# Squares behind the first norm, the second norm's product behind more tiles, rotation tables inside the FFN

## The chip, the cores and the metric

The kernel runs on 1 core of one Trainium2 chip. The metric is the time of one execution in device microseconds (us), taken as the median of several runs; lower is better. TensorE (PE) is shown with one of two granted clock levels, 1.2 and 2.4 GHz; a granted clock of 1.00 in a table means 2.4 GHz throughout, 0.50 would mean 1.2 GHz throughout.

## What is computed

Two transformer blocks follow each other on a sequence of 512 tokens with 1024 features, each with two layers, and each layer is a mixer and then a feed-forward part (FFN). Both parts have a norm ahead of them and a norm behind them, so between any two parts stands the same pair: the post-norm of what the part gave, added to the stream `x`, and the pre-norm of `x` for the next part.

```python
h = rms_norm(x, mix_norm_pre[l]) * (1.0 + sc_m) + sh_m
y = hybrid_mixer(h, positions, ...)
x = x + g_m * rms_norm(y, mix_norm_post[l])
h = rms_norm(x, ffn_norm_pre[l]) * (1.0 + sc_f) + sh_f
y = swiglu(h, w_gate_up[l], w_down[l])
x = x + g_f * rms_norm(y, ffn_norm_post[l])
```

The second block does the same without the scale and shift, with another mixer (`hybrid_mixer_2`) and a convolution in its FFN. `rms_norm` divides by the root of the mean square over the 1024 features. Both mixers rotate queries and keys by tables of cosine and sine of the positions; the second block has positions of its own (`positions_2`).

## The kernel before

Features lie on the 128 partitions, so `x` is eight tiles `x[k]` of 128x512, and tokens lie along the row. A weight is loaded in pieces of 128x1024 (`load`, L257 to L268): SyncE issues a DMA into `raw` (4 buffers), ScalarE rounds it to `whi` (L265), VectorE subtracts to get the rest, `wlo` (L267); there are four buffers each of `whi` and `wlo`. Every product of a weight and an activation is three matmuls: high by high, high by low, low by high.

At a boundary between two parts the work is cut into two halves of 256 tokens (A and B, `HALVES`). The last product of a part (`out_proj` for a mixer, `down2` for an FFN) runs its first output tiles whole and the others by half (`in_halves`): all of them for half A, then in reverse order for half B. So half A is done first and its norms can run while PE works on half B. The next part starts with `fm_split`: some output tiles for half A, then the same tiles for half B. The places where the norms stand between these tiles are given by small numbers at the top of the file: `LA` (mixer to FFN) and `LB` (FFN to mixer) say before which of the half-B tiles half A's pre-norm stands; `LC` (FFN) and `LD` (mixer) say before which half-A tile of the next part half B's pre-norm stands. A half-A or half-B tile of `out_proj` or `fm_split` is 24 matmuls, one of `down2` 33.

`post_norm` (L475) sums the squares of `y` over the partitions by a product with a matrix of ones (`nrm`), takes the root on ScalarE (`rstd`), and VectorE makes `yn` and adds it to `x`. `pre_norm` (L437) squares `x` on ScalarE (L444), adds pairs on VectorE (L446), has four products with ones on PE, takes the root, and then makes `xn` (VectorE), `hh` (ScalarE) and `hl` (VectorE), eight of each, which the next part's matmuls read. `rope_tables` (L544) makes the rotation tables: for the second block it is called right ahead of the FFN of the first block's second layer.

A scheduler puts the recorded instructions of each engine in an order by its own reckoning; on the chip each engine then runs its row as it stands and waits on semaphores. There are seven such boundaries with a following part: four from a mixer to an FFN, three from an FFN to a mixer.

Of the kernel before, what the change touches and what calls it, by code (L numbers as in the profile page):

```python
# [13 lines left out]
AF = mybir.ActivationFunctionType  # L14
ALU = mybir.AluOpType
# [6 lines left out]
KT = D // P  # L22
# [16 lines left out]
PD1 = 0  # L39
PD2 = 0  # L40
EARLY = 6
PAIRS = 4
PH1 = 0
PH2 = 0
PXM = 0
SA = 0
LA = 2
LAG = 3
LOA = 40
NO = 7  # L50
LB = 1
LC = 4
LD = 2
WIN = 0
KF = 3
KM = 1
# [20 lines left out]
HALVES = (slice(0, 256), slice(256, 512))  # L77
# [31 lines left out]
def steps(it, n):  # L109
    for _ in range(n):  # L110
        next(it, None)
        yield


def seq(*parts):
    for p in parts:
        yield from p
# [12 lines left out]
def run(steps):  # L130

    while True:
        try:
            dbg(steps)
            next(steps)
        except StopIteration as e:
            return e.value
# [49 lines left out]
class Net:  # L187
# [174 lines left out]
    def norms(self, y, sqs, g, nxt, late):  # L362


        if nxt is None:
            steps = [lambda i=i: self.post_norm(HALVES[i], y, sqs, g, True) for i in range(2)]
            return {0: steps[0]}, steps[1], (None, None)
        h = self.new_h()
        post = [lambda i=i: self.post_norm(HALVES[i], y, sqs, g) for i in range(2)]
        pre = [lambda i=i: self.pre_norm(HALVES[i], *nxt, *h) for i in range(2)]  # L370
        self.pending = pre[1]
        if late == 0:
            return {0: lambda: (post[0](), pre[0]())}, post[1], h
        return {0: post[0], late: pre[0]}, post[1], h

    def fm_split(self, chunks, act, pool, more=None):

        tiles = [self.ps("pj" if i < PJ else "ps") for i, _ in enumerate(chunks)]  # L380

        begin = {LC if more is None else LD: self.pending}
        middle = {} if more is None else {0: lambda: run(steps(more, 4))}
        self.in_halves([(i, [src]) for i, src in enumerate(chunks)], KF if more is None else KM,
                       lambda i, ws, hs, _: self.fm(tiles[i], ws[0], 0, act, hs, range(KT)), pool,
                       begin, middle)
        return tiles
# [46 lines left out]
        run(self.tok_steps(*args))  # L434


    def pre_norm(self, hs, gs, sh, hh, hl):  # L437

        nc, x = self.nc, self.x
        ps = self.ps("nrm")  # L440
        sq = None
        for k in range(KT):
            s2 = self.half("sq")
            nc.scalar.activation(s2, x[k][:, hs], AF.Square)  # L444
            if sq is not None:
                nc.vector.tensor_tensor(s2, sq, s2, ALU.add)  # L446

            sq = s2 if k < 2 * PAIRS and k % 2 == 0 else None
            if sq is None:
                self.matmul(ps[:, :256], self.ones, s2, start=k == min(1, PAIRS), stop=k == KT - 1)  # L450
        r = self.half("rstd")
        self.ln_exp_rstd(ps[:, :256], r, D)
        ts = []
        for k in range(KT + LAG):
            if k < KT:
                t = self.half("xn")
                ts.append(t)
                nc.vector.scalar_tensor_tensor(t, x[k][:, hs], gs[:, k:k + 1], r, ALU.mult, ALU.mult)
                if sh is None:
                    nc.scalar.activation(hh[k][:, hs], t, AF.Copy)  # L460
                else:
                    nc.scalar.activation(hh[k][:, hs], t, AF.Identity, bias=sh[:, k:k + 1])
            if k >= LAG:
                j = k - LAG
                lo, hi = hl[j][:, hs], hh[j][:, hs].bitcast(F32)
                pool = (PH2 if sh is None else PH1) >> j & 1
                if sh is None:
                    (nc.gpsimd if pool else nc.vector).tensor_tensor(lo, ts[j], hi, ALU.subtract)
                elif pool:
                    nc.scalar.activation(ts[j], ts[j], AF.Identity, bias=sh[:, j:j + 1])  # L470
                    nc.gpsimd.tensor_tensor(lo, ts[j], hi, ALU.subtract)
                else:
                    nc.vector.scalar_tensor_tensor(lo, ts[j], sh[:, j:j + 1], hi, ALU.add, ALU.subtract)
# [19 lines left out]
    def out_proj(self, chunks, act, y, g, nxt, pool):  # L493
# [19 lines left out]
        self.unspill()  # L513
        middle, end, h = self.norms(y, (ss, last), g, nxt, LA)
        self.in_halves([(f, [src for _, src in chunks(f)]) for f in range(KT - ntail, KT)], KO, one, pool, {}, middle)
# [26 lines left out]


    def rope_tables(self, pos):  # L544
        nc = self.nc
        cos = self.cp.tile([P, T], F32, tag="cos", name=self.nm("cos"))
        sin = self.cp.tile([P, T], F32, tag="sin", name=self.nm("sin"))
        pi = self.unit("pi", I32)
        nc.sync.dma_start(pi, pos.broadcast_to([P, T]))
        ang = self.unit("ang")  # L550
        nc.vector.tensor_copy(ang, pi)
        nc.vector.tensor_scalar(ang, ang, self.invf, None, ALU.mult)
        for tab, turn in ((sin, 0.0), (cos, 0.25)):
            n = self.unit("n")
            nc.vector.tensor_scalar(n, ang, 1.0 / TWO_PI, turn, ALU.mult, ALU.add)
            nc.vector.tensor_scalar(n, n, MAGIC, None, ALU.add)
            nc.vector.tensor_scalar(n, n, MAGIC, None, ALU.subtract)
            r = self.unit("r")
            nc.vector.scalar_tensor_tensor(r, n, -C1, ang, ALU.mult, ALU.add)
            nc.vector.scalar_tensor_tensor(r, n, -C2, r, ALU.mult, ALU.add)  # L560
            nc.vector.scalar_tensor_tensor(r, n, -C3, r, ALU.mult, ALU.add)
            if turn:
                nc.vector.tensor_scalar(r, r, math.pi / 2, None, ALU.add)
            nc.vector.tensor_scalar(r, r, PI_IN, -PI_IN, ALU.min, ALU.max)
            self.act(tab, r, AF.Sin)
        self.cos, self.sin = cos, sin

    def rope(self, pa, pb, n=P):
# [504 lines left out]
    def down2(self, chunks, act, y, g, nxt, pool):  # L1073
# [16 lines left out]
        self.use(LN_EXP)  # L1090
        middle, end, h = self.norms(lambda k, cs: y[k][:, cs], (ss, last), g, nxt, LB)
        self.in_halves([(f, [src for _, src in chunks(f)]) for f in range(KT - ntail, KT)], KD, one, pool, {}, middle)
# [3 lines left out]
    def block1(self, upto=None):  # L1096
        nc, A = self.nc, self.A
        par = []
        self.mod = []
        for l in range(2):  # L1100
            p = self.cp.tile([P, N1], F32, tag=f"par1_{l}", name=f"par1_{l}")
            nc.sync.dma_start(p, A["par1"][l])

            s = slice(B1["ml_out"], B1["ml_out"] + 4)
            nc.vector.tensor_scalar(p[:, s], p[:, s], 0.5, None, ALU.mult)
            par.append(p)
            self.mod.append(self.cp.tile([P, 48], F32, tag=f"mod{l}", name=f"mod{l}"))
        self.par = par
        self.hones = self.cp.tile([P, P], F32, name="hones")
        nc.vector.memset(self.hones, 0.0)  # L1110
        nc.vector.memset(self.hones[0:64, 0:64], 1.0)
        nc.vector.memset(self.hones[64:128, 64:128], 1.0)
        self.cact = self.cp.tile([P, D], F32, tag="shared", name="cact")
        nc.sync.dma_start(self.cact, A["c"].broadcast_to([P, D]))
        self.act(self.cact, self.cact, AF.Silu)
        h = self.new_h()
        for l in range(2):
            h = self.mix1(l, h, (self.modc(l, 4), self.modc(l, 3)), self.first(*h) if l == 0 else None)
            if upto == (1, l, "mix"):
                return  # L1120
            if l == 0:
                self.back = seq(self.modulation(0, (5,)), self.modulation(1, (0, 1, 2, 3, 4, 5)))
            nxt = (self.modc(1, 1), self.modc(1, 0)) if l == 0 else (self.par2c(0, "mix_pre"), None)

            def evict(f, pg, pu):
                t = self.unit("sg")
                self.act(t, pg, AF.Silu)
                nc.vector.tensor_tensor(t, t, pu, ALU.mult)
                return t

            if l == 1:
                self.rope_tables(A["positions_2"])
            gu, dn = A["w1_gu"][l], A["w1_dn"][l]
            h = self.ffn(h, lambda f, i: gu[2 * f + i], evict, lambda f, p: self.down_chunks(dn, f, p), self.modc(l, 5), nxt, (PF1, PD1))
            if upto == (1, l, "ffn"):
                return
        return h
# [597 lines left out]
```

## Time and profile before

| what | value |
|---|---|
| median of 3 runs | 3197.48 us (3195.8 to 3197.76) |
| the profiled execution | 3197.12 us, its span 3195.4 us |
| mean granted clock of PE | 0.978 |
| PE busy | 3044.9 us, 95% of the span |
| VectorE (DVE) busy | 2013.8 us, 63% |
| ScalarE (ACT) busy | 1548.1 us, 48% |
| chain that ended last | PE 70%, DVE 10%, ACT 3%, DMA 3% |

The span goes from the first instruction to the last, so the execution has 1.72 us around it. A row of the timeline gives start, length, engine, line, operation, output and inputs, and in brackets how long the engine was idle before it and for whom it waited. A row of the table of stretches gives the busy time of PE in the stretch, its instructions, the granted clock, the share of the DMA engines and GB/s. Matmuls overlap, so the length of a single one is no measure of what it costs; starts are.

### The profile page before, as it was taken

What the parts mean: (1) busy time and instruction counts of PE and PEld (TensorE: products, weight loads), DVE (VectorE), ACT (ScalarE), POOL (GpSimd) and SP (SyncE); (2) the same over time, 40 slices, a digit from 0 to 9 for tenths busy, and PEclk for the clock granted to TensorE, in tenths of its full rate; (3) what the DMA queues carried; (4) which work ended last, traced back from release to release, by engine and by line L of the source; (5) the groups of instructions that cost most, each with busy time, mean ns of one, the idle gap of its engine ahead of it and who ended that gap; (6) DMA issues with size and microseconds to landing.
All of it is one profiled execution on the core that took longest, in us unless ns stands there. A gap on an engine that the chain in (4) does not pass through costs nothing.

```text
span 3195.4 us, 42599 instructions
## 1 busy us (share of the span) xinstructions
PE 3044.9 (95%) x16196; PEld 2545.4 (80%) x16196; DVE 2013.8 (63%) x3692; ACT 1548.1 (48%) x2760; POOL 67.1 (2%) x179
## 2 busy tenths in 40 slices
PE   8998899998999899999999999999989999999998
PEld 6764788888875788888988779888888877898887
DVE  7887575546786563236676677635577766776365
ACT  4435542234445642234477665434445866454343
POOL 0000000000000000000000100000000001000000
PEclk9998999999999999999999999999999999999999
DMA  7244266644331232324421124333243112332323
GB/s 240 88 158 154 95 220 195 208 133 147 110 99 59 93 109 81 114 84 136 132 67 40 60 73 146 103 99 102 89 158 109 40 47 73 112 126 79 113 87 108
DMA packets 118925, 358.40 MB, mean 112 GB/s; under 512 B 15408, under 2 KB 28464, under 8 KB 118720
## 3 DMA queue, kind: packets, MB, share of 16 engines
q1 hardware_dynamic: 118720, 355.68, 34.2%
q8 instruction: 127, 2.08, 0.3%
q14 instruction: 78, 0.64, 0.1%
HBM read 336.19 MB, written 8.42 MB: 108 GB/s over the span
## 4 chain that ended last, share of the span: by engine, by line
PE 70%; issue 13%; DVE 10%; ACT 3%; DMA 3%; POOL 1%; SPq 0%; POOLq 0%; DVEq 0%; ACTq 0%
PE ps L305 28%; PE op L305 12%; PE pj L305 11%; PE dn L305 7%; PE tk L305 3%; PE po L305 2%; PE nrm L305 2%; DMA wm<-in_w_mod_dram 2%; DVE wlo L267 2%; DVE yn L488 1%; PE pt L308 1%; DVE x L489 1%; DVE wm L633 1%; DVE ss L1479 1%; PE cmp L305 1%
## 5 line engine op out<-in xcount | busy, mean ns | idle before, releaser
L267 DVE TENSOR_TENSOR wlo<-raw,whi 128x1024 fp32r<-128x1024 f32 (+1 forms) x562 | 628.7, 1123 | 577.8 <-ACT whi L265 575.4
L265 ACT ACTIVATE whi<-raw 128x1024 fp32r<-128x1024 f32 (+1 forms) x562 | 550.2, 980 | 803.3 <-PE ps L305 199.4
L305 PE MATMUL ps<-hh,whi 128*128 128x512 f32 (+1 forms) x1560 | 574.2, 368 | 0.0
L305 PE MATMUL ps<-hh,wlo 128*128 128x512 f32 (+1 forms) x1560 | 573.2, 367 | 0.0
L305 PE MATMUL ps<-hl,whi 128*128 128x512 f32 (+1 forms) x1560 | 572.5, 367 | 0.0
L305 PE MATMUL pj<-hh,whi 128*128 128x512 f32 (+1 forms) x944 | 352.8, 375 | 14.6 <-ACT hh L654 8.3
L305 PE MATMUL pj<-hl,whi 128*128 128x512 f32 (+1 forms) x944 | 351.5, 372 | 0.7 <-DVE hl L655 0.7
L305 PE MATMUL pj<-hh,wlo 128*128 128x512 f32 (+1 forms) x944 | 350.7, 371 | 0.1
L305 PEld LDWEIGHTS ps<-hh,wlo 128*128 128x128 f32 x1560 | 295.3, 189 | 48.8 <-DVE wlo L267 0.6
L305 PEld LDWEIGHTS ps<-hh,whi 128*128 128x128 f32 x1560 | 295.6, 189 | 48.1
L305 PEld LDWEIGHTS ps<-hl,whi 128*128 128x128 f32 x1560 | 295.3, 189 | 47.9
L305 PEld LDWEIGHTS pj<-hh,whi 128*128 128x128 f32 x944 | 179.5, 191 | 54.1 <-ACT hh L654 10.6
L305 PEld LDWEIGHTS pj<-hh,wlo 128*128 128x128 f32 x944 | 179.7, 190 | 30.3 <-issue 1.2
L305 PEld LDWEIGHTS pj<-hl,whi 128*128 128x128 f32 x944 | 179.8, 190 | 29.6 <-DVE hl L655 1.7
L633 DVE CUSTOM_DVE_ANT_0 wm<-wm,cact 128x1024 f32<-128x1024 f32 x96 | 116.9, 1221 | 108.4 <-DMA wm<-in_w_mod_dram 108.2
L305 PE MATMUL op<-hidh,whi 128*128 128x256 f32 (+1 forms) x572 | 178.5, 312 | 0.0
L305 PE MATMUL op<-hidh,wlo 128*128 128x256 f32 (+1 forms) x572 | 177.1, 310 | 0.3 <-DVE wlo L267 0.3
L305 PE MATMUL op<-hidl,whi 128*128 128x256 f32 (+1 forms) x572 | 176.5, 309 | 0.0
L305 PE MATMUL dn<-hidl,whi 128*128 128x512 f32 x352 | 137.0, 389 | 0.1
L305 PE MATMUL dn<-hidh,wlo 128*128 128x512 f32 x352 | 136.9, 389 | 0.0
L305 PE MATMUL dn<-hidh,whi 128*128 128x512 f32 x352 | 136.9, 389 | 0.0
L275 ACT ACTIVATE p<-p,st 128x128 f32<-128x128 f32 (+3 forms) x192 | 106.2, 556 | 57.7 <-DVE st L872 38.7
(350 smaller groups left out, 5804.0 us busy)
## 6 DMA issues: line engine op xcount, KB each, us to landing
raw<-in_w_in_dram SPq DMA_DIRECT2D x134, 512.0 KB, 3.4
raw<-in_w_up_dram SPq DMA_DIRECT2D x100, 512.0 KB, 3.5
wm<-in_w_mod_dram SPq DMA_DIRECT2D x96, 512.0 KB, 4.6
raw<-in_w_gu_dram SPq DMA_DIRECT2D x94, 512.0 KB, 3.5
raw<-in_w_dn_dram SPq DMA_DIRECT2D x80, 512.0 KB, 3.5
raw<-in_w_out_dram SPq DMA_DIRECT2D x52, 512.0 KB, 3.6
raw<-in_w_dn_dram SPq DMA_DIRECT2D x80, 192.0 KB, 3.1
hp<-rp SPq DMA_DIRECT2D x96, 64.0 KB, 2.0
```

The source lines that it names most:

```text
L265: nc_.scalar.activation(hi[:, :n], raw[:, :n], AF.Copy)
L267: (self.lo_eng or nc_.vector).tensor_tensor(lo[:, :n], raw[:, :n], hi[:, :n].bitcast(F32), ALU.subtract)
L275: j = self.nc.scalar.activation(out, in_, func, **kw).ins
L305: return self.paced(self.nc.tensor.matmul(*args, **kw))
L308: return self.paced(self.nc.tensor.transpose(*args))
L488: nc.vector.scalar_tensor_tensor(t, y(k, hs), g[:, k:k + 1], r, ALU.mult, ALU.mult)
L489: (nc.gpsimd if PXM >> k & 1 else nc.vector).tensor_tensor(self.x[k][:, hs], self.x[k][:, hs], t, ALU.add)
L633: self.nc.vector.tensor_tensor_reduce(raw, raw, self.cact, 1.0, 0.0, ALU.mult, ALU.add, self.mod[l][:, c:c + 1])
L1479: nc.vector.tensor_tensor_scan(s[:, c][:, ::-1], a[:, c][:, ::-1], a[:, c][:, ::-1], 0.0, ALU.add, ALU.bypass)
```

## The change

The squares of `x` for a half (ScalarE) and their sums by pairs (VectorE) leave `pre_norm` and become a function `squares`, which is called right behind that half's `post_norm`; `pre_norm` is given their results. Half A's pre-norm moves from before the third half-B tile to before the fifth (`LA` 2 to 4), at an FFN's end from before the second to before the fourth (`LB` 1 to 3). Half B's pre-norm in an FFN's first tiles moves from before the fifth to before the sixth and last half-A tile (`LC` 4 to 5). In a mixer it moved with `LD`: it stood before the third half-A tile, and now stands behind all of them (three in the first block, four in the second), in the first block behind one tile of the token-wise product (`tk`) as well. The rotation tables of the second block are no longer made in one go ahead of the FFN; a generator makes them in six steps that the FFN's `tick` calls one by one. The number of instructions stays, but for two table loads on ScalarE that are gone (2535 rows before, 2533 after).

```diff
-LA = 2
+LA = 4
-LB = 1
-LC = 4
-LD = 2
+LB = 3
+LC = 5
...
-        post = [lambda i=i: self.post_norm(HALVES[i], y, sqs, g) for i in range(2)]
-        pre = [lambda i=i: self.pre_norm(HALVES[i], *nxt, *h) for i in range(2)]
-        self.pending = pre[1]
-        if late == 0:
-            return {0: lambda: (post[0](), pre[0]())}, post[1], h
-        return {0: post[0], late: pre[0]}, post[1], h
+        sq = {}
+
+        def post(i):
+            self.post_norm(HALVES[i], y, sqs, g)
+            sq[i] = self.squares(HALVES[i])
+
+        pre = lambda i: self.pre_norm(HALVES[i], sq[i], *nxt, *h)
+        self.pending = lambda: pre(1)
+        return {0: lambda: post(0), late: lambda: pre(0)}, lambda: post(1), h
...
-        begin = {LC if more is None else LD: self.pending}
-        middle = {} if more is None else {0: lambda: run(steps(more, 4))}
+        def between():
+            early = 4 - len(chunks)
+            run(steps(more, early))
+            self.pending()
+            run(steps(more, 4 - early))
+
+        begin, middle = ({LC: self.pending}, {}) if more is None else ({}, {0: between})
...
+    def squares(self, hs):
+
+        nc, x, res = self.nc, self.x, []
         for k in range(KT):
             s2 = self.half("sq")
             nc.scalar.activation(s2, x[k][:, hs], AF.Square)
-            if sq is not None:
-                nc.vector.tensor_tensor(s2, sq, s2, ALU.add)
...
+            if k % 2:
+                nc.vector.tensor_tensor(s2, res[-1], s2, ALU.add)
+                res.pop()
+            res.append(s2)
+        return res
+
+    def pre_norm(self, hs, sqs, gs, sh, hh, hl):
...
+        for i, sq in enumerate(sqs):
+            self.matmul(ps[:, :256], self.ones, sq, start=i == 0, stop=i == len(sqs) - 1)
...
             if l == 1:
-                self.rope_tables(A["positions_2"])
+                self.back = self.rope_steps(A["positions_2"])
```

ScalarE at the first boundary from a mixer to an FFN, from the second half-B tile on. `op` is the tile's product, `y` and `sqy` its eviction and square, `whi` a weight's rounding, `sq` a square of `x`. Before:

```order
L265 ACTIVATE whi_3688<-raw_3687 128x1024
L506 ACTIVATE sqy_3490<-op_3464 128x256
L504 ACTIVATE y_3122<-op_3493 128x256
L506 ACTIVATE sqy_3519<-op_3493 128x256
L444 ACTIVATE sq_3523<-x_3159 128x256
L444 ACTIVATE sq_3525<-x_3160 128x256
```

and now:

```order
L263 ACTIVATE whi_3695<-raw_3694 128x1024
L448 ACTIVATE sq_3471<-x_3166 128x256
L448 ACTIVATE sq_3473<-x_3167 128x256
L448 ACTIVATE sq_3476<-x_3168 128x256
L448 ACTIVATE sq_3478<-x_3169 128x256
L448 ACTIVATE sq_3481<-x_3170 128x256
L448 ACTIVATE sq_3483<-x_3171 128x256
L448 ACTIVATE sq_3486<-x_3172 128x256
L448 ACTIVATE sq_3488<-x_3173 128x256
L516 ACTIVATE sqy_3517<-op_3491 128x256
L514 ACTIVATE y_3129<-op_3520 128x256
```

The eight squares moved ahead of three evictions and squares of `y`; the weight's rounding still stands ahead of them.

PE at the first boundary from an FFN to a mixer, where half A's pre-norm has its products with ones (`nrm`), between tiles of the down product (`op`). Before:

```order
L305 MATMUL op_6539<-hidh_6089,wlo_6469 128x256
L305 MATMUL nrm_6577<-sq_6580,ones 128x256
L305 MATMUL nrm_6577<-sq_6586,ones 128x256
L305 MATMUL nrm_6577<-sq_6592,ones 128x256
L305 MATMUL nrm_6577<-sq_6598,ones 128x256
L305 MATMUL op_6649<-hidh_5346,whi_6638 128x256
```

and now:

```order
L303 MATMUL op_6616<-hidh_6096,wlo_6612 128x256
L303 MATMUL op_6666<-hidh_5353,whi_6655 128x256
L303 MATMUL op_6666<-hidl_5354,whi_6655 128x256
L303 MATMUL nrm_6704<-sq_6548,ones 128x256
L303 MATMUL nrm_6704<-sq_6553,ones 128x256
L303 MATMUL op_6666<-hidh_5353,wlo_6656 128x256
L303 MATMUL op_6666<-hidh_5429,whi_6655 128x256
```

Before, one half-B tile stood ahead of the four products; now two tiles and two matmuls stand ahead of the first two, and the other two follow 31 matmuls later, with two tiles behind them instead of four.

ScalarE at the same boundary, from half A's pre-norm root (`rstd`) on, where `hh` is made. Before:

```order
L275 ACTIVATE rstd_6602<-rstd_6602 128x256
L462 ACTIVATE hh_6245<-xn_6605,mod_122 128x256
L462 ACTIVATE hh_6246<-xn_6608,mod_122 128x256
L462 ACTIVATE hh_6247<-xn_6611,mod_122 128x256
L265 ACTIVATE whi_6738<-raw_6737 128x1024
L462 ACTIVATE hh_6248<-xn_6614,mod_122 128x256
L265 ACTIVATE whi_6744<-raw_6743 128x384
L462 ACTIVATE hh_6249<-xn_6618,mod_122 128x256
L462 ACTIVATE hh_6250<-xn_6622,mod_122 128x256
```

and now:

```order
L273 ACTIVATE rstd_6709<-rstd_6709 128x256
L472 ACTIVATE hh_6252<-xn_6712,mod_122 128x256
L472 ACTIVATE hh_6253<-xn_6715,mod_122 128x256
L263 ACTIVATE whi_6918<-raw_6917 128x1024
L472 ACTIVATE hh_6254<-xn_6718,mod_122 128x256
L263 ACTIVATE whi_6948<-raw_6947 128x1024
L472 ACTIVATE hh_6255<-xn_6721,mod_122 128x256
L263 ACTIVATE whi_6978<-raw_6977 128x1024
L472 ACTIVATE hh_6256<-xn_6725,mod_122 128x256
L263 ACTIVATE whi_7009<-raw_7008 128x1024
L472 ACTIVATE hh_6257<-xn_6729,mod_122 128x256
```

Between the `hh` now stand four roundings of whole pieces, those of the mixer's first weights, where before pieces of 1024 and 384 columns of the down product alternated.

## Rows read from the trace of the kernel before

**Rows 1.** The page's group of weight rests on VectorE (count | busy, mean ns | idle, releaser)

```profile
L267 DVE TENSOR_TENSOR wlo<-raw,whi 128x1024 fp32r<-128x1024 f32 (+1 forms) x562 | 628.7, 1123 | 577.8 <-ACT whi L265 575.4
```

**Rows 2.** Who PE waited for: us in total, times, longest

```profile
PE nrm L305 <- DVE sq L446: 48.3, 11, 7.1
```

**Rows 3.** Timeline of PE at the first boundary of either kind, half A's pre-norm

```profile
375.45 3.78 PE L305 MATMUL nrm<-sq,ones 128*128 128x256 f32 x8 [3.74 <-DVE sq L446]
...
752.39 3.78 PE L305 MATMUL nrm<-sq,ones 128*128 128x256 f32 x8 [5.78 <-DVE sq L446]
```

**Rows 4.** Stretches of PE, 7 us from the end of each wait: busy, clock, DMA

```profile
375.45:382.45 7.00, 7.00 (x28) 0.57 0.44 151
752.39:759.39 7.00, 7.00 (x34) 0.68 0.35 103
782.75:789.75 7.00, 7.00 (x38) 0.76 0.73 253
1103.12:1110.12 7.00, 7.00 (x30) 0.62 0.47 150
1141.81:1148.81 7.00, 7.00 (x34) 0.70 0.00 0
1488.52:1495.52 7.00, 7.00 (x30) 0.60 0.33 103
1519.07:1526.07 7.00, 7.00 (x29) 0.58 0.82 283
1957.97:1964.97 7.00, 7.00 (x38) 0.76 0.46 150
2332.99:2339.99 7.00, 7.00 (x35) 0.69 0.36 105
2362.92:2369.92 7.00, 7.00 (x52) 1.00 0.71 253
2798.50:2805.50 7.00, 7.00 (x40) 0.79 0.47 150
```

**Rows 5.** Timeline of VectorE, ScalarE and PE, first boundary from mixer to FFN, half A

```profile
372.51 0.75 DVE L489 TENSOR_TENSOR x<-x,yn 128x256 f32<-128x256 f32 x2
...
373.39 2.56 ACT L444 ACTIVATE sq<-x 128x256 f32<-128x256 f32 x8
...
388.95 1.83 DVE L473 SCALAR_TENSOR_TENSOR hl<-xn,mod,hh 128x256 fp32r<-128x256 f32 x4
...
394.49 0.28 PE L305 MATMUL pj<-hh,whi 128*128 128x256 f32 x1
```

**Rows 6.** A stretch of PE: one half-A tile of 24 matmuls in the FFN

```profile
408.66:411.53 2.87, 2.87 (x25) 1.00 0.77 261
```

**Rows 7.** Timeline, first boundary from FFN to mixer, half A

```profile
749.45 0.75 DVE L489 TENSOR_TENSOR x<-x,yn 128x256 f32<-128x256 f32 x2
...
756.21 0.48 ACT L275 ACTIVATE rstd<-nrm,eps 128x256 f32<-128x256 f32 x1 [2.78 <-PE nrm L305]
...
765.86 1.66 DVE L473 SCALAR_TENSOR_TENSOR hl<-xn,mod,hh 128x256 fp32r<-128x256 f32 x4
...
772.20 0.28 PE L305 MATMUL pj<-hh,whi 128*128 128x256 f32 x1
```

**Rows 8.** Timeline, first boundary from mixer to FFN, half B

```profile
407.12 1.89 PE L305 MATMUL nrm<-sq,ones 128*128 128x256 f32 x8
...
409.99 1.28 ACT L288 ACT_TABLE_LOAD   x1
...
414.76 1.66 DVE L473 SCALAR_TENSOR_TENSOR hl<-xn,mod,hh 128x256 fp32r<-128x256 f32 x4
```

**Rows 9.** Timeline of ScalarE at the boundary with the rotation tables

```profile
1140.12 0.63 ACT L275 ACTIVATE sin<-r 128x512 f32<-128x512 f32 x1 [7.05 <-DVE r L564]
```

**Rows 10.** Stretches of PE with short waits in the second block's mixers

```profile
1776.70:1783.70 7.00, 5.71 (x27) 0.76 0.24 75
...
2617.77:2624.77 7.00, 5.36 (x31) 1.00 0.23 75
```

More of the change, by code (lines that the diff above doesn't have):

```diff
@@ L41 @@
 EARLY = 6
-PAIRS = 4
 PH1 = 0
@@ L434, in tok @@
         run(self.tok_steps(*args))
[L437 to L441, printed above, removed]
+    def squares(self, hs):
+        nc, x, res = self.nc, self.x, []
         for k in range(KT):
@@ L444, in pre_norm @@
             nc.scalar.activation(s2, x[k][:, hs], AF.Square)
-            if sq is not None:
-                nc.vector.tensor_tensor(s2, sq, s2, ALU.add)
-            sq = s2 if k < 2 * PAIRS and k % 2 == 0 else None
-            if sq is None:
-                self.matmul(ps[:, :256], self.ones, s2, start=k == min(1, PAIRS), stop=k == KT - 1)
+            if k % 2:
[4 more added lines that the diff above has]
+    def pre_norm(self, hs, sqs, gs, sh, hh, hl):
+        nc, x = self.nc, self.x
+        ps = self.ps("nrm")
+        for i, sq in enumerate(sqs):
+            self.matmul(ps[:, :256], self.ones, sq, start=i == 0, stop=i == len(sqs) - 1)
         r = self.half("rstd")
@@ L544, in rope_tables, with rope_steps @@
     def rope_tables(self, pos):
+        run(self.rope_steps(pos))
+    def rope_steps(self, pos):
         nc = self.nc
@@ L557, in rope_tables @@
             nc.vector.tensor_scalar(n, n, MAGIC, None, ALU.subtract)
+            yield
             r = self.unit("r")
@@ L561, in rope_tables @@
             nc.vector.scalar_tensor_tensor(r, n, -C3, r, ALU.mult, ALU.add)
+            yield
             if turn:
@@ L565, in rope_tables @@
             self.act(tab, r, AF.Sin)
+            yield
         self.cos, self.sin = cos, sin
```

## The prediction

> **What bounds the kernel now.** I read the table of engines first: PE is busy 95% of the span and no other engine comes near, so only time in which PE stands, or runs at a lower clock, can be won. Next the list of whom PE waited for: 48.3 us in 11 waits go to one pair, a boundary's product with ones (`nrm`) behind a pair sum of squares (`sq`) from VectorE [rows 2]. Then the timeline of PE at the boundaries, to see the pattern: half A's pre-norm waits 3.74 us from a mixer to an FFN and 5.78 us from an FFN to a mixer [rows 3]. With four boundaries of the first kind and three of the second that makes 4 x 3.74 + 3 x 5.78 = 32.3 us. The other 16.0 us are half B's, at the four starts of [rows 4] that are not half A's: 782.75, 1141.81, 1519.07 and 2362.92. The one at 1141.81 is the longest, 7.1 us; ScalarE stood 7.05 us there because VectorE was making the rotation tables [rows 9]. Its three fellows share 8.9 us, about 3.0 each.
>
> A wait costs more than its length. The stretches of 7 us behind the eleven waits show PE busy without a break at a granted clock of 0.57 to 0.79 in nine cases, 0.76 in one and 1.00 in one [rows 4], so part of them ran at 1.2 GHz. The clock is 1.00 where nothing stood before [rows 6]. The sum of (1 - clock) over the eleven is 3.25, and 3.25 x 7 = 22.8 us. What hangs on these waits is therefore 48.3 + 22.8 = 71.1 us, 2.2% of the time.
>
> **The change part by part.**
>
> *Half A, mixer to FFN (four times).* PE would be at the product at 375.45 - 3.74 = 371.71. Two more tiles now stand ahead of it, 2 x 2.87 = 5.74 us [rows 6], so it is there at 377.45. The last `x` was ready at 373.26 and the squares took until 375.95 [rows 5], on a ScalarE where they still stand behind a rounding of a weight; issuing them earlier brings little, the later product does the work. The wait goes, and so does its clock loss, (1 - 0.57) x 7 = 3.0 us [rows 4]. The product is no earlier for that: begun at 377.45 at full clock (1.89 us [rows 8], against 3.78 [rows 3]) it ends at 379.34, before 379.23. So `rstd` and the eight `hl` stay where they are, the last ending near 390.8 [rows 5], while PE reaches the FFN's first `pj` 6.7 us sooner, at 387.8 instead of 394.49 [rows 5]. The last `hl` is needed only at the 22nd of the first tile's 24 matmuls, 2.5 us in, at 390.3. The slack of 6.2 us that stood here before is used up: a new wait of 0 to 0.6 us; I take 0.4.
>
> *Half B, mixer to FFN (four times).* Its product is one tile later. Before, it did not wait, and its last `hl` ended 9.3 us behind the product's start, the table load of 1.28 us among it [rows 8]. Half B's first tiles take their k steps in turn, so the last `hl` is needed late; I take 0.15 us. For all eight halves: 4 x 0.4 + 4 x 0.15 = 2.2 us. From above I put 1.5 each: the 0.4 and one whole weight rest of 1.12 us [rows 1] between the `hl`. That is 12 us.
>
> *Half A, FFN to mixer (three times).* Without its wait PE is at the old place at 752.39 - 5.78 = 746.61. One tile of 33 matmuls (33/24 x 2.87 = 3.9 us) and two matmuls later it meets the first two products, near 750.7. The last `x` is ready at 750.2 [rows 7], but the first two products read only the first pair sums, and the other two stand 31 matmuls (3.6 us) further. Then `rstd` ends near 756.6, as before (756.69 [rows 7]). The mixer's first `pj` moves from 772.20 by 5.78 + (1 - 0.68) x 7 = 8.0 us to 764.2, and its last `hl` is needed about 38 matmuls into two tiles that alternate, at 768.6. When is it there? If the distance from `rstd` stays at 11 us [rows 7], near 767.8: no wait. But between the `hh` now stand four whole pieces instead of whole ones and pieces of 384 columns in turn. Two pieces grow from some 0.42 to 1.12 us on VectorE [rows 1], 1.4 us, and the third and fourth need buffers which the last down tiles still read. My walk along both engines puts the end near 770.4, a wait of 1.8 us. If all four pieces came on top (4 x 1.12 = 4.5 us), it would be near 4. I take 1.8, the walk's value: 3 x 1.8 = 5.4 us, bounds 0 and 12.
>
> *Half B, FFN to mixer (three times).* The product now stands behind all half-A tiles. PE no longer waits for the sums, but whole tiles are fewer behind it: in the first block's second mixer two of the token-wise ones. I take 0.5 us each and 0.5 more there, 2.0 us; the upper bound is that the old 3.0 us return, 9 us.
>
> *The clock behind new waits.* Short waits need not cost clock: a stretch with 1.29 us of idle time shows 0.76, one with 1.64 us shows 1.00 [rows 10]. One drop costs (1 - 0.76) x 7 = 1.7 us; half of the three longest waits gives 2.5 us. If six of them drop, it is 10.
>
> *The rotation tables.* Seventeen rows of VectorE leave the boundary, and with them the wait of 7.05 us on ScalarE [rows 9]. They go behind the first FFN tile's products, where VectorE is busy 63% on the whole and PE has no gaps. The two sines run under the table that is loaded there, and two table loads go, about 1.3 us each [rows 8], on an engine that has the time. Moved too is the DMA of the positions: it stands on SyncE's queue behind three raw weights, and the cast of them stands on VectorE early, with gates and weight rests queued behind it, which PE waits for. Three pieces of 128x1024 in four bytes are 1.57 MB, 6 us at the 261 GB/s of [rows 6]; but a piece feeds one output tile, two times 24 matmuls or 5.7 us, and four stand in buffers, 23 us of cover. I take 0, at most 6, which the upper bounds below have room for. The raw weights of the part that follows keep their order.
>
> *The sum.* Given back: 2.2 + 5.4 + 2.0 + 2.5 = 12.1 us, bounds 0 and 12 + 12 + 9 + 10 = 43. Net 71.1 - 12.1 = 59.0. Against the profiled execution, 3197.12, that is 3138.1; the median is 0.36 higher, so **3138.5 us**.
>
> **The rivals.** *Everything goes and nothing comes back:* 3197.5 - 71.1 = 3126.4. For it: at both kinds of boundary `hl` is within 2 us of being in time. Against it: in both kinds of half A the slack is gone by the same working. Chance 0.12.
>
> *The wait moves to `hl`:* a part's first `pj` wait for the last `hl`, for the reasons above, at their upper bounds: 43 us back, 3169.5. It holds if the roundings between the `hh` stand in wait for buffers that PE frees late. Against it: rows of before show whole pieces in this chain already without a wait behind it. Chance 0.14.
>
> *Many short waits, each with a drop of the clock:* fourteen halves, each with one drop of 1.7 us as at 1776.70 [rows 10], give 14 x 1.7 = 24 us back instead of 2.5, so 3138.5 + 21 = 3160. Against it speaks 2617.77, a longer idle time with a clock of 1.00 [rows 10]. The Trainium skill, "TensorE: Matmul & The Clock Gate", section "A second HAM failure mode: psum-queue depth-cycling", tells of a kernel whose clock went up and down because PE idled for moments between groups of matmuls, and lost throughput that way; by it the two rows would read 0.76 both, and they do not agree. Chance 0.08.
>
> *It does not do what it says:* if ScalarE reaches the squares no sooner and PE waits at the later place for the same time, it is 3197. The two tiles put between (5.74 against 3.74) speak against it. Chance 0.04.
>
> *Slower:* the squares now stand on ScalarE ahead of three evictions and squares of `y`. ScalarE takes its row in order, so it stands in them until VectorE has the last `x`, as it stood 7.05 us for the tables [rows 9]; evictions queue behind it and PE finds no free psum. If in all fourteen halves PE stood that long with one clock drop of 1.7 us each, 14 x 8.75 = 122 us come in and 71 go: 51 more, 3248. It becomes slower from 71/14 = 5.1 us a half. Against it: `x` of half A is complete at 373.26 [rows 5], about when ScalarE gets there, and the tiles behind it have buffers of their own. Chance 0.04.
>
> **How the numbers follow.** The forecast of 3138.5, 3130 to 3148 by itself, has 0.58. The measurement can tell about 0.2%, 6.4 us, from no change. Faster by more than that: 0.58 + 0.12 + 0.14 + 0.08 = 0.92; the same 0.04; slower 0.04. The range goes from just under the full gain, 3124, to just short of all upper bounds together, 3168; out of it lie the two last rivals and the upper part of the second, some 0.15.
>
> **What would show it.** PE's waits for `sq` from VectorE should be gone from the list, and the granted clock near 1.00 behind each boundary. New should be waits of PE's `pj` for `hl` or `hh`, of 1 to 2 us at the three boundaries from an FFN to a mixer, and next to none at the four others. ScalarE's `sin` should show no wait of 7 us, and two table loads fewer. The prediction is wrong if an eviction or a psum tile (a wait of PE for `y`) turns up at the boundaries, or PE waits for `wlo` in the FFN where the positions are cast.

## The result and the profile after

The changed kernel takes 3139.68 us (median of 4 runs, 3138.26 to 3144.87), the kernel before 3196.64 us beside it; the ratio is 0.9825, with a 95% interval of 0.9809 to 0.984. The forecast was 3138.5 us, with a range of 3124 to 3168.

The top of the page of the changed kernel: span; busy time, share and instructions of each engine; then the two rows of 40 slices of the span that are PE's busy tenths and its granted clock.

```profile
span 3139.1 us, 42582 instructions
PE 3033.7 (97%) x16196; PEld 2533.5 (81%) x16196; DVE 2012.8 (64%) x3692; ACT 1545.5 (49%) x2758; POOL 66.7 (2%) x179
...
PE   7998999999999999999999999999999999999998
...
PEclk8997999999998999999999999999999999999999
```

PE's instructions are the same in number, their busy time is 11 us shorter at a mean granted clock of 0.984 against 0.978, and ScalarE has two instructions fewer, the table loads.

Whom PE waited for, in the rows of that list which belong to the boundaries (us in total, times, longest):

```profile
PE pj L303 <- DVE hl L478: 3.4, 5, 0.9
...
PE nrm L303 <- DVE sq L450: 1.9, 3, 0.7
...
PE pj L303 <- DVE hl L483: 1.7, 2, 0.9
...
PE op L303 <- DVE wlo L265: 1.4, 4, 0.3
```

The 48.3 us of [rows 2] have become 1.9. In their place stand 5.1 us of waits for `hl`, and 0.34 us for a weight rest at each FFN's end, which the kernel before had only at its last one. The timeline of PE at the places of [rows 3], and on to the first `pj` (start, length, operation; in brackets the idle time before it):

```profile
381.30 1.89 PE L303 MATMUL nrm<-sq,ones 128*128 128x256 f32 x8
...
391.66 0.28 PE L303 MATMUL pj<-hh,whi 128*128 128x256 f32 x1
...
752.80 1.02 PE L303 MATMUL nrm<-sq,ones 128*128 128x256 f32 x4
...
761.57 0.28 PE L303 MATMUL pj<-hh,whi 128*128 128x256 f32 x1
...
764.14 0.39 PE L303 MATMUL pj<-hl,whi 128*128 128x256 f32 x1 [0.73 <-DVE hl L483]
...
766.06 0.39 PE L303 MATMUL pj<-hl,whi 128*128 128x256 f32 x1 [0.95 <-DVE hl L483]
...
777.07 1.13 PE L303 MATMUL nrm<-sq,ones 128*128 128x256 f32 x4 [0.71 <-DVE sq L450]
```

At the four boundaries from a mixer to an FFN nothing waits any more in this profile. At the first from an FFN to a mixer half A's last `hl` are late by 1.68 us in two pieces, and half B's sums by 0.71.

Stretches of PE of 7 us behind these places (busy time, count, granted clock, DMA), to set beside [rows 4]:

```profile
375.50:382.50 7.00, 7.00 (x56) 1.00 0.34 117
382.50:389.50 7.00, 7.00 (x59) 1.00 0.57 186
764.14:771.14 7.00, 6.05 (x44) 1.00 0.52 163
777.07:784.07 7.00, 6.77 (x46) 1.00 0.54 189
1475.05:1482.05 7.00, 5.36 (x38) 1.00 0.68 241
1489.95:1496.95 7.00, 7.00 (x52) 1.00 0.70 252
2304.59:2311.59 7.00, 6.11 (x45) 1.00 0.44 159
```

The clock is 1.00 in all of them, also where PE stood for up to 1.64 us within the stretch.

**Where the 57 us lie.** Take as marks the first `op<-cl` of the first mixer and the product with the last `sql`, in the timeline of PE now

```profile
343.55 0.50 PE L303 MATMUL op<-cl,whi 128*128 128x512 f32 x1 [0.87 <-DVE cl L253]
...
3128.64 0.70 PE L303 MATMUL nrm<-sql,ones 128*128 128x256 f32 x2 [0.53 <-ACT sql L1100]
```

and before:

```profile
339.55 0.50 PE L305 MATMUL op<-cl,whi 128*128 128x512 f32 x1 [0.86 <-DVE cl L255]
...
3184.93 0.70 PE L305 MATMUL nrm<-sql,ones 128*128 128x256 f32 x2 [0.53 <-ACT sql L1084]
```

Between them the trace is 60.3 us shorter. PE's busy time in this stretch, for the kernel before, the changed kernel and a second profile of it (run eight below):

```profile
339.55:3184.93 2845.38, 2754.90 (x14928) 0.99 0.33 107
343.55:3128.64 2785.09, 2736.44 (x14929) 0.99 0.34 110
338.80:3125.99 2787.19, 2734.52 (x14929) 1.00 0.35 110
```

PE was busy for 18.5 us less (20.4 in the second profile) with the same matmuls (a record more or less), and idle for 41.8 us less (37.8). In front of the first mark the change moves nothing, yet the profile of after is 4.0 us longer there. In the fourteen profiles of this case that stretch ends between 338.80 and 345.26, whatever the kernel, so it is a difference of executions.

### The profile page after: what moved, and what is told of

Read it like the earlier page. It is cut to its first block, busy times and chain, and to the rows that moved or that the text cites. A ratio compares the mean times of both kernels' runs of the same rounds, so it can differ in the third digit from the quotient of the medians.

```text
span 3139.1 us, 42582 instructions
## 1 busy us (share of the span) xinstructions
PE 3033.7 (97%) x16196; PEld 2533.5 (81%) x16196; DVE 2012.8 (64%) x3692; ACT 1545.5 (49%) x2758; POOL 66.7 (2%) x179
## 4 chain that ended last, share of the span: by engine, by line
PE 68%; issue 17%; DVE 10%; ACT 3%; DMA 1%; POOL 1%; SPq 0%; POOLq 0%; DVEq 0%; ACTq 0%
PE ps L303 29%; PE op L303 12%; PE pj L303 9%; PE dn L303 8%; PE po L303 3%; PE tk L303 2%; DVE wlo L265 2%; PE nrm L303 1%; PE pt L306 1%; DVE yn L498 1%; DVE ss L1495 1%; DVE x L499 1%; DVE ia L846 1%; ACT whi L263 1%; DVE m L845 1%
```

## The experiments

Twelve runs follow, four on each of three chips (one to four, five to eight, nine to twelve); the kernel before was timed on each chip beside them, and a ratio is to those times. For comparison inside a trace I use the stretch between the two marks: 2845.4 us in the kernel before, 2785.1 and 2787.2 in two profiles of the changed kernel.

**One: the tables alone.** The kernel before, with the generator `rope_steps` of the changed kernel and

```diff
-                self.rope_tables(A["positions_2"])
+                self.back = self.rope_steps(A["positions_2"])
```

> The kernel before with only the rotation tables made inside the FFN. My theory: the wait of 7.13 us at that boundary goes, and the 2.1 us of clock behind it, and nothing comes back in the FFN: 9.2 us off, 3187.4 us, and no wait of PE longer than 1 us in the FFN where the positions are cast. Rival: the cast and the seventeen rows hold up weight rests in the FFN, and PE waits there for wlo: 3190 to 3197 us.

3188.93 us against 3198.62, ratio 0.9966 (0.9953 to 0.9979); between the marks 9.2 us less. The wait at 1141.81 is gone from the list (41.1 us in 10 waits stay), and no wait for `wlo` came up in the FFN. The cast did have to wait for its DMA, in the changed kernel by 1.50 us, without a trace on PE (VectorE and ScalarE, changed kernel):

```profile
1146.48 0.43 DVE L564 CAST ang<-pi 128x512 f32<-128x512 int32 x1 [1.50 <-DMA pi<-in_positions_dram]
...
1153.66 0.62 ACT L273 ACTIVATE sin<-r 128x512 f32<-128x512 f32 x1
```

**Two: the tables back, the rest changed.**

```diff
-                self.back = self.rope_steps(A["positions_2"])
+                self.rope_tables(A["positions_2"])
```

> The changed kernel with the rotation tables made in one go at the boundary again. My theory: one more tile (2.9 us) stands ahead of half B's product now, so the wait there is 7.1 - 2.9 = 4.2 us and costs 2 us of clock: 3146 us. Rival: the new order covers the tables by itself and that part of the change is worth nothing in it: 3139 to 3141 us.

3151.82 us against 3198.62, ratio 0.9848 (0.9831 to 0.9865): 12 us above the changed kernel by the times, 7.2 and 5.1 us above its two profiles between the marks. The size was wrong: PE waits 9.27 us, longer than the 7.13 before, and not for `sq`. ScalarE and PE of this kernel tell why:

```profile
1113.32 2.55 ACT L448 ACTIVATE sq<-x 128x256 f32<-128x256 f32 x8
1124.35 0.63 ACT L273 ACTIVATE sin<-r 128x512 f32<-128x512 f32 x1 [8.47 <-DVE r L579]
1127.32 0.63 ACT L273 ACTIVATE cos<-r 128x512 f32<-128x512 f32 x1 [2.35 <-DVE r L579]
1127.97 1.28 ACT L286 ACT_TABLE_LOAD   x1
1129.27 0.47 ACT L273 ACTIVATE rstd<-nrm,eps 128x256 f32<-128x256 f32 x1
...
1132.06 1.01 PE L303 MATMUL ps<-hh,whi 128*128 128x256 f32 x3 [9.27 <-ACT hh L472]
```

The squares are done at 1115.87 and PE's product with ones runs at 1118.0 without a wait, but `rstd` and `hh` stand behind the two sines on ScalarE, which stand for VectorE. Early squares cover nothing of that (run three, with the places as before, shows 8.76 us for `hh` here); the wait only moves from the product to the first matmul that reads `hh`.

**Three and four: the squares alone, the places alone.** Three is the changed kernel with `LA`, `LB`, `LC`, `LD` and the order in `fm_split` as before and the tables in one go; four has the new places, and the squares made at the product, tables in one go:

```diff
-            sq[i] = self.squares(HALVES[i])
...
-        pre = lambda i: self.pre_norm(HALVES[i], sq[i], *nxt, *h)
+        pre = lambda i: self.pre_norm(HALVES[i], self.squares(HALVES[i]), *nxt, *h)
```

> The squares issued right behind the post-norm, all the places of the pre-norms and the tables as before. My theory (the later product does the work): the squares start about 0.7 us sooner at each half, the list keeps some 43 us of waits of PE for sq, 3192 us. Rival (the early squares do the work): the waits for sq are nearly gone, about 3140 to 3150 us.

> The pre-norms at their new places, but the squares made inside them as before, and the tables as before. The prediction's sentence (the later product does the work, issuing the squares earlier brings little) gives: waits for sq gone in both kinds of half A, some 50 us off, about 3148 us. Rival (neither does it alone): ScalarE has the squares behind the evictions of the tiles that now stand ahead, so they start later by as much as the product does, the waits of 3.7 and 5.8 us stay and fewer tiles are left behind them for hh and hl: 3190 to 3210 us.

| kernel (tables in one go) | median, us | ratio to before (95%) | between the marks, to before | PE's waits for `sq` |
|---|---|---|---|---|
| squares early alone | 3195.46 | 0.9986 (0.9974 to 0.9997) | -9.9 us | 33.1 us, 10 |
| places late alone | 3186.30 | 0.9953 (0.9936 to 0.9969) | -12.8 us | 32.1 us, 11 |
| both (run two) | 3151.82 | 0.9848 (0.9831 to 0.9865) | -53.1 us | 1.9 us, 3 |

For three, the time is near the 3192 us of my theory, though its waits for `sq` are 33 us and not 43: the long one at the tables has become the wait for `hh` of 8.76 us, and the others are shorter by 8 us. For four, both sides expected wrong: the waits at half A stay, as the rival had it, but shorter (2.96 and 2.8 us), so it is 12 us faster and not level. Neither edit does it alone, and together they take off 53 us where the parts sum to 23. At the first boundary, the rows of the places alone (VectorE's last `x`, ScalarE, PE):

```profile
375.10 0.76 DVE L498 TENSOR_TENSOR x<-x,yn 128x256 f32<-128x256 f32 x2
...
380.95 0.37 ACT L513 ACTIVATE y<-op 128x256 f32<-128x256 f32 x1
381.21 0.38 ACT L515 ACTIVATE sqy<-op 128x256 f32<-128x256 f32 x1
381.48 2.55 ACT L447 ACTIVATE sq<-x 128x256 f32<-128x256 f32 x8
...
383.02 1.22 PE L303 MATMUL nrm<-sq,ones 128*128 128x256 f32 x2 [2.96 <-DVE sq L449]
```

and of the changed kernel:

```profile
376.50 0.75 DVE L499 TENSOR_TENSOR x<-x,yn 128x256 f32<-128x256 f32 x2
...
376.59 2.55 ACT L448 ACTIVATE sq<-x 128x256 f32<-128x256 f32 x8
```

With the places alone `x` is complete at 375.86, but the squares begin at 381.48, 5.6 us later, because ScalarE has them behind the evictions (`y`, `sqy`) of the two tiles that now stand ahead of the product. The product moved back and took its squares with it. In the changed kernel they begin as `x` comes in. With the squares alone they begin early too, but PE is at the product before the sums: 3.08 us four times, 3.98 three times.

**Five, six, seven, nine: one place put back at a time**, in the changed kernel: `LA` 4 to 2; `LB` 3 to 1; half B's pre-norm in a mixer before the third half-A tile (`LD` 2); `LC` 5 to 4. Eight is the changed kernel again.

```diff
-LA = 4
+LA = 2
```

> The changed kernel with half A's pre-norm in an FFN's front again before the third half-B tile (LA 2); squares early, all else changed. My theory now (early squares and later product are needed together): as with the squares alone, four waits of 3.1 us for sq, 12.3 us, and 0 to 3 us of clock behind each: 3152 to 3164 us, most likely 3157. Rival (with the squares early the place is worth nothing at this boundary): 3138 to 3142 us, no waits for sq here.

```diff
-LB = 3
+LB = 1
```

> The changed kernel with half A's pre-norm at an FFN's end again before the second half-B tile (LB 1). My theory: three waits of 4.0 us for sq, 12 us, and 2.8 us of clock behind each; the new waits for hl (5.0 us in all) go: 12 + 8 - 5 = 15 us more, 3155 us. Rival (the roundings between the hh cost as much as the later product wins): 3138 to 3144 us.

```diff
-        begin, middle = ({LC: self.pending}, {}) if more is None else ({}, {0: between})
+        begin = {LC if more is None else LD: self.pending}
+        middle = {} if more is None else {0: lambda: run(steps(more, 4))}
```

> The changed kernel with half B's pre-norm in a mixer before the third half-A tile again (LD 2), all else changed. My theory: the three waits of half B return at 2.5 to 3.1 us instead of 0.6 to 0.7, 6.8 us more, with 3 us of clock: 3150 us. Rival (the early squares alone remove them): 3138 to 3142 us.

> The changed kernel itself once more, on the chip of the three runs beside it. My theory: 3136 to 3142 us; the profile before the first boundary between two parts (which the change does not touch) differs by some us from the other profiles, and PE's waits behind it are those of the profile after, to 0.1 us.

```diff
-LC = 5
+LC = 4
```

> The changed kernel with half B's pre-norm in an FFN's first tiles one tile sooner again (LC 4), where the kernel before showed no wait. My theory: the last pair sum is there at 406.5 in the profile after and the product at 406.9, so one tile sooner (2.9 us) PE waits some 2 us for sq at three or four boundaries, 8 us, with 0 to 3 us of clock each: 3148 us. Rival (this part was not needed, the kernel before had no wait here): 3138 to 3142 us.

| put back | median, us | above the changed kernel (3139.98 in run eight) | between the marks, us (2785.1 and 2787.2 with nothing put back) | PE's waits for `sq`, us |
|---|---|---|---|---|
| `LA` | 3160.95 | 21.0 | 2801.8 | 14.0 (four of 3.08) |
| `LB` | 3145.38 | 5.4 | 2795.4 | 12.7 (three of 3.98); none for `hl` at half A |
| half B in the mixer | 3165.62 | 25.6 | 2810.2 | 19.2 (6.47, 6.36, 6.36) |
| `LC` | 3141.70 (another chip) | 1.7 | 2788.5 | 2.4 (two of 0.26 new) |

Two of the four places are needed by the times: the ratio intervals of `LA` (0.986 to 0.9893) and of half B in the mixer (0.9875 to 0.9903) lie apart from run eight's (0.9795 to 0.9823). For `LB` (0.9811 to 0.984) they overlap, so the times do not show it; between the marks its profile is 8 to 10 us longer, and its waits for `sq` are there. `LB` gave less than I expected, 5.4 us and not 15, nearer to the rival. The 15 had the end of the waits for `hl` in it already. The three waits of 3.98 us came as priced, but with those for `hl` went half B's waits for `sq` (1.9 us) and the weight rests of 0.34 us (1.0 us in all), and PE's busy time between the marks is only 5 to 7 us longer where I had put 8. `LA` came out in its range. `LC` gave nothing that can be measured: my expectation of 2 us of waits took the distance from the trace of after as fixed, but one place earlier the sums came earlier too, and 0.26 us at two boundaries remain.

Run eight, 3139.98 us, came as expected, with 4.75 us less in front of the first mark than the profile of after. Its waits are not the same to 0.1 us, though: those for `hl` at the second boundary from an FFN to a mixer are 1.63 us and not 2.04, a new one of 0.20 us for `hl` stands at the first boundary, and away from the boundaries PE waits 1.8 us for `hidh` and 1.0 us for `ss` that the profile of after does not have.

The surprise is half B in the mixer. I expected the 2.5 to 3.1 us of the kernel before to come back, and it was 6.4. Rows of this kernel, VectorE and PE, and PE's clock behind the three waits:

```profile
765.21 1.66 DVE L479 SCALAR_TENSOR_TENSOR hl<-xn,mod,hh 128x256 fp32r<-128x256 f32 x4
...
774.82 0.75 DVE L495 TENSOR_TENSOR x<-x,yn 128x256 f32<-128x256 f32 x2
...
775.96 3.88 PE L304 MATMUL nrm<-sq,ones 128*128 128x256 f32 x8 [6.47 <-DVE sq L446]
```

```profile
775.96:782.96 7.00, 7.00 (x33) 0.67 0.50 179
1495.48:1502.48 7.00, 7.00 (x30) 0.62 0.50 188
2330.87:2337.87 7.00, 7.00 (x27) 0.55 0.51 187
```

Half B's chain on VectorE begins only when half A's last `hl` is done (766.87), and that chain did not keep up with PE: counted from the first mark, the last `hl` is done 2.2 us sooner than in the kernel before (425.8 against 428.0), the mixer's first `pj` 13.3 us sooner (419.3 against 432.6). PE no longer stands in half A, comes to half B's product sooner and stands there. 19.2 us of waits and (0.33 + 0.38 + 0.45) x 7 = 8.1 us of clock, less the 1.9 of after, make 25.4, and 25.6 were measured (25.1 and 23.0 between the marks). A part of what half A gains would have been given back one step later without the new place of half B.

**Ten to twelve: a better place at an FFN's end?** Ten has `LB` 2, eleven keeps `LB` 3 and raises the scheduler's priority of half A's `xn`, `hh` and `hl`, twelve does both:

```diff
-        for k in range(KT + LAG):
...
+        with self.tc.high_priority(pri):
+            for k in range(KT + LAG):
...
```

> The changed kernel with half A's pre-norm at an FFN's end one tile sooner (LB 2, between the old 1 and the new 3). My theory: the product meets PE about when the last pair sum is there, a wait of 0 to 1.5 us for sq, and rstd and the hl come some 3 us sooner, so that the waits for hl of 1.7, 2.0 and 1.3 us go; no clock is lost behind waits this short: 3136 to 3140 us, in the trace 0 to 1.5 us less at each of the three boundaries. Rival: the wait for sq is as long as with LB 1, 4 us: 3145 us.

> The changed kernel with xn, hh and hl of half A put ahead of other work by priority in the scheduler at an FFN's end; the places as in the changed kernel. One piece of the old part's weight rest (0.55 us) leaves the stretch between the first xn and the last hl, the four whole ones stay. My theory: the waits for hl become 0.5 us shorter each, 1.5 us in all, which the times cannot show: 3136 to 3141 us. Rival (the order of hh and hl decides): the waits for hl gone.

> Both: the pre-norm one tile sooner (LB 2) and its xn, hh and hl by priority. My theory: waits for hl gone, the wait for sq as with LB 2 alone: 3135 to 3139 us. Rival: as LB 2 alone.

3139.93, 3141.21 and 3140.95 us, with ratios of 0.9813 (0.98 to 0.9827), 0.9822 and 0.982: none can be told from the changed kernel. With `LB` 2 the waits for `hl` at half A are gone and there is none for half A's `sq`, as forecast, but half B's sums of squares of `x` are now 1.58 us late at each of the three boundaries instead of 0.6 to 0.7, and ahead of that PE waits some 1.4 us for half B's sums of squares of `y` (`ssy`), which it did not before. Their rows in the list of waits:

```profile
PE nrm L303 <- DVE sq L450: 4.7, 3, 1.6
...
PE nrm L303 <- DVE ssy L1102: 4.2, 3, 1.5
```

The priority left the waits for `hl` where they were (3.0 and 2.0 us in the list, 3.4 and 1.7 in after), so the 0.5 us at each boundary that I expected of it did not come. Twelve fell out otherwise than either side expected: with the priority the waits for `hl` are back (3.0 and 2.0 us), though `LB` is 2, and the wait for half B's `sq` is 0.9 to 1.0 us; why was not followed. What is left at these boundaries, some 2 to 3 us each, moved between `hl`, `ssy` and `sq` and did not shrink.

## Why the prediction held, and where it did not

**What hung on the waits** (48.3 us and 22.8 us of clock): held for the waits, some 2 to 4 us too high for the clock. The waits for `sq` fell from 48.3 us in 11 to 1.9 in 3, and the clock is 1.00 where they stood; but PE's busy time between the marks fell by 18.5 us in one profile and 20.4 in the other, not by 22.8. At the first boundary of the first kind `pj` was forecast 6.7 us sooner; measured from the first mark it is 54.94 us before and 48.11 now, 6.8 us. From there to the mixer's first `pj` it was to be 8.0 us and is 377.71 - 369.91 = 7.8.

**What was given back** (12.1 us): 7.1 by the waits of after. Term by term, forecast and measured: mixer to FFN 2.2 and 0; half A's `hl` at the FFN's end 5.4 and 5.0 (1.68, 2.04 and 1.30); half B there 2.0 and 2.1; the clock 2.5 and 0. So the walk along both engines was right to some tenths for the mixer. Two terms were too high, the one from mixer to FFN and the clock behind short waits. At the first boundary from mixer to FFN the last `hl` was done 50.4 us behind the first mark where 51.25 was forecast, 0.36 us ahead of the matmul that reads it.

The 2.5 us of clock, and the rival of many drops with it, came of a misreading of [rows 10]: their 1.29 and 1.64 us of idle time lie inside the stretches, but both stretches begin right behind a longer wait, which stands ahead of them (timeline of PE, kernel before):

```profile
1776.70 0.55 PE L308 MATMUL pt<-ident,ss 128*128 128x128 f32 x3 [2.56 <-ACT ss L275]
...
2617.77 0.55 PE L308 MATMUL pt<-ident,ss 128*128 128x128 f32 x3 [2.52 <-ACT ss L275]
```

So the clocks of 0.76 and 1.00 stand behind waits of 2.5 us and told nothing of the new waits, of which none is above 0.95 us.

With 7.1 us given back, 64 us net, the time would have been 3133.5; the marks show 60.3 and 58.2 us in two profiles. PE's busy time, which has the clock of the whole stretch in it, fell by 4.3 and 2.4 us less than 22.8; with the weight rests of 0.34 us (1 us) and, in the second profile, the waits of some 3 us away from the boundaries, that is the difference to within 2 us. That the forecast lies 1.2 us from the median is therefore in part luck: it had too much for what was lost and too much for what comes back, and the two errors nearly cancel. From the first mark to the first `op<-cl` of the second mixer the two profiles of the changed kernel take 712.8 and 715.9 us, so a single profile does not settle some 3 us.

**The tables** (cost 0, gain 9.2): held, by run one 9.2 us between the marks. In the new order they would have been waited for longer, 9.27 us, by run two.

**The sentence that fell** is the one on half A from mixer to FFN: "issuing them earlier brings little, the later product does the work". The sum was right, since it priced both edits together, but its attribution was not. I had read that the squares still stand behind a rounding and begin only some tenths sooner. That compared them with the old place of the product. At the new place they would have begun 39.3 us behind the first mark, as run four shows, and with the edit they begin at 33.0, 6.3 us sooner: without it they move with the product.

**Half B in the mixer** was taken as a leftover with an upper bound of the old 3.0 us. At the place that the change has, 0.6 to 0.7 us came, as forecast. But the working took the old wait to be the worst that half B could bring. Run seven measured 6.4 us at the old place: the wait grew when half A became faster, which the prediction did not see.

**The rivals.** Full gain: not reached. `hl` at its upper bounds: the waits are there, at 5 us in all and not 12. Many short waits with a clock drop each: the two profiles of the changed kernel have 22 waits of 0.2 to 0.95 us for `hl`, `hh` and `sq` at the boundaries, and the clock is 1.00 behind all of them. The Trainium skill, "TensorE: Matmul & The Clock Gate", section "A second HAM failure mode: psum-queue depth-cycling", tells of a kernel whose clock went up and down because PE idled for moments between groups of matmuls; behind these 22 waits the trace shows nothing of the kind. No change at all: the times are 57 us apart. Slower, by evictions behind the squares: PE shows no wait for an eviction at a boundary.

## What to carry over

Where a wait is removed by moving its consumer later, look at what is recorded together with the consumer: work that is issued from the same function moves along, and the producer stays as late as it was. Price the consumer's place and the producer's place as a pair, and each alone, before giving the credit to one. Where two chains follow each other on one engine, time won at the first wait can be waited for at the second, as in run seven, so the second place has to be looked at too. And before a clock is read as what short waits cost, look at the wait that stands ahead of the stretch.

## What the runs showed of the hardware

The clock behind a wait differed with its length, and not smoothly. In the profiles of before and of runs one to eight, all 27 waits of 3.7 us or more at a boundary are followed by 7 us with a granted clock of 0.55 to 0.79. Of the 24 waits of 2.5 to 3.2 us eight are followed by a clock of 1.00 and sixteen by 0.56 to 0.78, the same wait of the same kernel sometimes one and sometimes the other. The first boundary and the other three of run five, each behind a wait of 3.08 us:

```profile
378.44:385.44 7.00, 7.00 (x39) 0.76 0.48 151
1095.07:1102.07 7.00, 7.00 (x52) 1.00 0.49 152
1925.82:1932.82 7.00, 7.00 (x38) 0.76 0.45 150
2757.96:2764.96 7.00, 7.00 (x38) 0.76 0.51 150
```

Behind the short waits of under 2 us for `sq`, `hl` and `hh` the clock was 1.00 (0.99 once), but for one place of run five (0.64 and 0.95 us, 0.76) and two that followed a wait of 3.98 us closely in run six. What decides between the cases in the middle was not tried.
